# Hybrid mLSTM, sparse attention and retention block: the low part of a weight chunk made by two engines, one k-tile each

## The chip, the cores and the metric

One core of one Trainium2 chip runs the whole program. Time is device time in microseconds (us) of one launch, median of three runs. The engines named here: PE does matmuls, DVE elementwise work, reductions and top-k steps, ACT activations and copies, POOL (GpSimd) elementwise work, and SP issues most DMAs.

## What is computed

Two layers on x of 512 tokens by 1024 features, all in float32. Cut to the sections that matter here:

```
z = rms_norm(x) @ w_in                       # split into q,k,v,i,f,o (mLSTM), latents (attention),
                                             # q,k,v,g (retention), three gates
hm = mlstm(silu(conv(q,k)), v, i, f)         # chunks of 128 tokens, a state carried along
idx = sum_g w_idx[g] * relu(q_idx[g] @ k_idx)    # 8 indexer heads; the top 128 keys of each query
ha = attention over the chosen keys, with a bucketed bias
hr = retention(rotary(q), rotary(k), v)      # chunks of 128, a state carried along
y = sig(g_m)*(hm@p_m) + sig(g_a)*(ha@p_a) + sig(g_r)*(hr@p_r)
x = x + y @ w_out;  x = x + (silu(h@w_gate) * (h@w_up)) @ w_down
```

## The kernel before

Activations stay on the chip; weights are streamed. Every product is made from a high and a low part of both factors, three matmuls for one (`mm3`, L251 to L253: high by high, high by low, low by high). A weight chunk is two k-tiles of 128 rows by up to 512 columns. `chunk` (L221 to L235) loads it from HBM into `raw` (two buffers) by a DMA that SP issues, lets ACT make the high part `whi` by a copy to the reduced float type (L233), and lets DVE subtract it from `raw` for the low part `wlo` (L234); `whi` and `wlo` have three buffers each. A full chunk feeds 24 matmuls of 512 columns.

The layer goes through sections of four chunks each (`feat_section`, `tok_section`): latents and gates first, then qk, mv (the values of the mLSTM), mo (its output gate), rq, rk, rv, rg of the retention, then the gates, output projections and the FFN. Work of other kinds is fed between the matmuls by generators (`during`, `tick`): the indexer runs beside qk and mv, `conv_silu` and `mlstm_gates` beside mv, `mlstm_pre` and `topk` beside mo, `mlstm` and `topk` beside rq to rg, `retention` from the first gate section on. The names for later: `qs` is an indexer query split in its high and low part (ACT L605, DVE L606), `relu` is ACT's evacuation of the indexer's scores (L629), `mask` the sum over heads (DVE L634); `topk` takes 16 rounds of MAX8 and MATCH_REPLACE8 over each of three masks (L649, L650) and ends a mask at L652; `msc` and `mst` (DVE L852, L862) belong to the mLSTM's steps, `rsc` (DVE L911) to the retention's; `sm` and `mm` are PSUM tiles. POOL multiplies gains (L468, L549, L550), and finishes rotary (L524, L525).

What stands in which order on an engine's queue is decided when the program is built: a scheduler walks an estimate of the program and takes the ready instruction of the highest priority. Weight chunks are made under high priority (`tc.high_priority` in `chunk`), the top-k rounds under a low one (`TOP_PRIO`). So a change of an instruction's size or engine also changes the order of others. Once built, each engine runs its queue strictly in order.

Of the kernel before, what the change touches and what calls it, by code (L numbers as in the profile page):

```python
# [11 lines left out]
F32 = mybir.dt.float32  # L12
# [91 lines left out]
class Block:  # L104
    def __init__(self, ctx, tc, a, depth):
        self.tc, self.nc, self.a, self.depth = tc, tc.nc, a, depth
        pool = lambda name, bufs, **k: ctx.enter_context(tc.tile_pool(name=name, bufs=bufs, **k))
        self.const = pool("const", 1)
        self.wp = pool("wp", 3)
        self.big = pool("big", 1)  # L110
        self.wk = pool("wk", 1)
        self.st = pool("st", 4)
        self.ps = pool("ps", 1, space=PSUM)
        self.dram = pool("dram", 1, space=DRAM)
        self.feed = []
        self.ahead = []
        self.late = []

    def tick(self):
        for f in self.feed:  # L120
            f[2] += f[1]
            while f[2] >= 1.0:
                f[2] -= 1.0
                next(f[0], None)
# [98 lines left out]
    def chunk(self, k0, kt, parts, width, offset=None):  # L223
        nc = self.nc
        with self.tc.high_priority(offset=offset):
            raw = self.wp.tile([128, 2, 512], F32, name="raw", tag="raw", bufs=2)
            hi = self.wp.tile([128, 2, 512], F32R, name="whi", tag="whi")
            lo = self.wp.tile([128, 2, 512], F32R, name="wlo", tag="wlo")
            for c0, src in parts:
                n = src.shape[1]  # L230
                nc.sync.dma_start(raw[:, 0:kt, c0:c0 + n], src.rearrange("(k p) c -> p k c", p=128))
            r, h, o = (t[:, 0:kt, 0:width] for t in (raw, hi, lo))
            nc.scalar.activation(h, r, AF.Copy)  # L233
            nc.vector.tensor_sub(o, r, h.bitcast(F32))  # L234
        return hi, lo  # L235

    def chunks(self, w, cols, rows=None):
# [138 lines left out]
    def mixer(self, l, act):  # L376
        nc, a = self.nc, self.a
# [46 lines left out]
        for h in range(4):  # L424
            o = 64 - 64 * (h % 2)
# [9 lines left out]
        def conv_silu():  # L435
            for f, z in enumerate(pre_conv):
# [12 lines left out]
                    nc.vector.tensor_mul(kT[f - 2], y, z)  # L449
                yield  # L450

        masks = {b: self.r(f"mask{b}", [128 * (b + 1)]) for b in range(1, NT)}
        idx = self.indexer(l, anorm, CT, wgt, masks)
        bias = self.bias_table() if l == 0 else iter(())
# [99 lines left out]
        ret = self.retention(rq, rk, rv, rg, hr)  # L554
        self.tok_section(w_in, ((C_RG, C_RG + 512),), act, ev_rg)
        self.drain(top)
        att = self.attention(l, CT, masks, haT)
        self.during((ret, 1.25))
        sg = gate(C_GM, 0)
# [279 lines left out]
    def mlstm(self, qz, kT, v1, og, hmT):  # L839
# [6 lines left out]
        def chunk(c):  # L846
# [39 lines left out]
            self.to_T(hx, hmT, c)  # L886

        yield from wave(chunk(c) for c in range(NT))

    def retention(self, rq, rk, rv, rg, hrT):  # L890
# [5 lines left out]
        def chunk(c):  # L896
# [38 lines left out]
            self.to_T(hx, hrT, c)  # L935

        yield from wave(chunk(c) for c in range(NT))

    def ffn(self, l, X, act):
# [94 lines left out]
```

## Time and profile before

| | us |
|---|---|
| three runs | 1827.42, 1827.93, 1828.56 (median 1827.93) |
| profiled execution | 1827.7 |
| its span | 1825.9 |
| TensorE clock granted | 0.999 of full speed over the span |

The profiled execution's own time is 1.8 us longer than its span. Rows of a timeline are one instruction or several alike in a run (x2), with the start in us from the beginning of the span and the time; a bracket gives the idle time of the engine ahead of it and what ended it. Two-input instructions are TENSOR_TENSOR and SCALAR_TENSOR_TENSOR. The figures of PE's matmuls overlap: a 512-column matmul shows as 0.39, and starts follow each other every 0.227 us.

### The profile page before, as it was taken

How to read it: one execution, taken by the hardware profiler on the slowest of the kernel's cores; microseconds unless marked ns; L12 is line 12 of the kernel's file. 1: busy time of each engine (PE TensorE's matmuls, PEld its weight loads, DVE VectorE, ACT ScalarE, POOL GpSimd, SP SyncE). 2: the span in 40 equal slices, each digit the busy share in tenths (PEclk: the TensorE clock that was granted, in tenths of full speed). 3: DMA queues.
4: the chain of work that ended last, by engine and by line, in shares of the span. 5: the costliest groups of instructions: out<-in, count | busy, mean ns of one | idle time of the engine just before them, and what ended most of it. 6: DMA issues, size and time to landing. Idle time of an engine off the chain costs nothing.

```text
span 1825.9 us, 22880 instructions
## 1 busy us (share of the span) xinstructions
PE 1796.5 (98%) x8720; PEld 1490.9 (82%) x8720; DVE 982.5 (54%) x1798; ACT 741.1 (41%) x1208; POOL 217.5 (12%) x274
## 2 busy tenths in 40 slices
PE   9999999999999999999999999999999999999998
PEld 6878888888888888888887788888888888888886
DVE  5698985455545333322357999744546443333223
ACT  5572235656434323322246523365654333223221
POOL 3112140121000000000020122301210000000000
PEclk9999999999999999999999999999999999999999
DMA  5622423222235333322342233232223253332232
GB/s 187 202 86 77 116 69 100 93 85 87 82 126 161 93 95 102 92 97 100 102 131 70 75 91 95 71 113 74 90 70 138 83 156 97 93 104 92 94 102 81
DMA packets 126845, 185.95 MB, mean 102 GB/s; under 512 B 12256, under 2 KB 71136, under 8 KB 126736
## 3 DMA queue, kind: packets, MB, share of 16 engines
q1 hardware_dynamic: 125408, 178.98, 31.4%
q0 software_dynamic: 1184, 5.26, 0.9%
q8 instruction: 68, 1.11, 0.2%
q14 instruction: 41, 0.34, 0.1%
q10 hardware_dynamic: 144, 0.26, 0.0%
HBM read 177.64 MB, written 6.84 MB: 101 GB/s over the span
## 4 chain that ended last, share of the span: by engine, by line
PE 78%; DVE 14%; ACT 3%; DMA 2%; issue 2%; POOL 1%; SPq 0%; POOLq 0%; ACTq 0%; DVEq 0%
PE mm L251 23%; PE mm L253 23%; PE mm L252 23%; DVE wlo L234 3%; DVE mask L650 3%; DVE top L649 2%; PE sm L731 2%; PE sm L710 1%; ACT whi L233 1%; PE sm L724 1%; DMA raw<-w_up 1%; DVE ru L523 1%; PE sm L369 1%; DVE mhx L362 0%; DMA uk<-a_wuk 0%
## 5 line engine op out<-in xcount | busy, mean ns | idle before, releaser
L234 DVE TENSOR_TENSOR wlo<-raw,whi 128x1024 fp32r<-128x1024 f32 (+2 forms) x302 | 374.2, 1239 | 590.6 <-ACT whi L233 590.3
L233 ACT ACTIVATE whi<-raw 128x1024 fp32r<-128x1024 f32 (+2 forms) x302 | 314.0, 1040 | 716.8 <-PE mm L252 300.8
L251 PE MATMUL mm<-hT,whi 128*128 128x512 f32 (+1 forms) x1216 | 465.9, 383 | 0.4 <-ACT rg L544 0.2
L252 PE MATMUL mm<-hT,whi 128*128 128x512 f32 (+1 forms) x1216 | 460.5, 379 | 1.0 <-DVE hT L304 1.0
L253 PE MATMUL mm<-hT,wlo 128*128 128x512 f32 (+1 forms) x1216 | 460.9, 379 | 0.0
L253 PEld LDWEIGHTS mm<-hT,wlo 128*128 128x128 f32 x1216 | 228.7, 188 | 43.1
L252 PEld LDWEIGHTS mm<-hT,whi 128*128 128x128 f32 x1216 | 229.0, 188 | 41.9 <-DVE hT L304 1.6
L251 PEld LDWEIGHTS mm<-hT,whi 128*128 128x128 f32 x1216 | 228.9, 188 | 41.7 <-ACT rg L544 0.8
L251 PE MATMUL mm<-whi,hT 128*128 128x512 f32 (+1 forms) x448 | 177.2, 396 | 2.0 <-ACT hT L303 1.3
L253 PE MATMUL mm<-whi,hT 128*128 128x512 f32 (+1 forms) x448 | 174.6, 390 | 0.0
L252 PE MATMUL mm<-wlo,hT 128*128 128x512 f32 (+1 forms) x448 | 174.1, 389 | 0.0
L251 PEld LDWEIGHTS mm<-whi,hT 128*128 128x128 f32 x448 | 84.1, 188 | 19.5 <-ACT hT L303 2.0
L253 PEld LDWEIGHTS mm<-whi,hT 128*128 128x128 f32 x448 | 84.1, 188 | 18.1 <-issue 1.2
L252 PEld LDWEIGHTS mm<-wlo,hT 128*128 128x128 f32 x448 | 84.2, 188 | 16.0 <-issue 0.5
L321 POOL TENSOR_SCALAR rs<-ms 128x1 f32<-128x1 f32 x16 | 5.7, 355 | 619.0 <-ACT hn L319 619.0
L251 PE MATMUL mm<-whi,fa 128*128 128x512 f32 x192 | 75.5, 393 | 0.0
L252 PE MATMUL mm<-wlo,fa 128*128 128x512 f32 x192 | 75.5, 393 | 0.0
L253 PE MATMUL mm<-whi,fa 128*128 128x512 f32 x192 | 75.4, 393 | 0.0
L712 POOL TENSOR_TENSOR cmb<-tb,mask 128x256 f32<-128x256 f32 (+2 forms) x48 | 51.4, 1074 | 161.2 <-PE sm L724 55.1
L251 PE MATMUL mm<-whi,fr 128*128 128x512 f32 x160 | 62.4, 390 | 0.0
L253 PE MATMUL mm<-whi,fr 128*128 128x512 f32 x160 | 62.3, 389 | 0.0
L252 PE MATMUL mm<-wlo,fr 128*128 128x512 f32 x160 | 62.3, 389 | 0.0
(286 smaller groups left out, 2654.7 us busy)
## 6 DMA issues: line engine op xcount, KB each, us to landing
raw<-w_in SPq DMA_DIRECT2D x104, 512.0 KB, 3.6
raw<-w_gate SPq DMA_DIRECT2D x96, 256.0 KB, 2.8
raw<-w_up SPq DMA_DIRECT2D x96, 256.0 KB, 3.1
raw<-w_down SPq DMA_DIRECT2D x44, 512.0 KB, 3.6
raw<-w_out SPq DMA_DIRECT2D x16, 512.0 KB, 3.6
x<-x SPq DMA_DIRECT2D x8, 512.0 KB, 6.4
rot<-c_rot SPq DMA_DIRECT2D x16, 256.0 KB, 3.2
tb<-bias_dram SPq DMA_DIRECT2D x16, 256.0 KB, 3.9
```

Of the source, the lines that this page charges most:

```text
L233: nc.scalar.activation(h, r, AF.Copy)
L234: nc.vector.tensor_sub(o, r, h.bitcast(F32))
L251: t.matmul(out, lhsT=A[0], rhs=B[0], start=start, stop=False)
L252: t.matmul(out, lhsT=A[0], rhs=B[1], start=False, stop=False)
L253: t.matmul(out, lhsT=A[1], rhs=B[0], start=False, stop=stop)
L369: self.nc.tensor.transpose(p[:, h, :], x[:, h, :], self.ident)
L523: nc.vector.tensor_mul(u, z, sin)
L649: nc.vector.max(m8, acc)
L650: nc.vector.match_replace(acc, m8, acc, TAKEN)
L710: nc.tensor.matmul(p, lhsT=q[v][:, b * 128:(b + 1) * 128], rhs=kk[v][:, 0:SP], start=v == 0, stop=v == 1)
L712: nc.gpsimd.tensor_add(c, tb[:, T - S:T], masks[b] if b else self.neg)
L731: nc.tensor.matmul(o[:, b, :], lhsT=PT[:, s, :], rhs=V[s][:, h * 64:(h + 1) * 64], start=s == 0, stop=s == b)
```

## The change

A flag `share` is set in each layer from before the qk section until the rg section has been issued. While it holds, a chunk of two k-tiles has its low part made in two instructions: DVE subtracts k-tile 0 (128x512), POOL subtracts k-tile 1 (128x512). That concerns 29 chunks of a layer, the four of each of seven sections and the indexer's own weights, 58 in all; the other chunks stay with one DVE instruction.

```diff
--- before.py
+++ after.py
@@ -115,6 +115,7 @@
         self.feed = []
         self.ahead = []
         self.late = []
+        self.share = False
 
     def tick(self):
         for f in self.feed:
@@ -231,7 +232,10 @@
                 nc.sync.dma_start(raw[:, 0:kt, c0:c0 + n], src.rearrange("(k p) c -> p k c", p=128))
             r, h, o = (t[:, 0:kt, 0:width] for t in (raw, hi, lo))
             nc.scalar.activation(h, r, AF.Copy)
-            nc.vector.tensor_sub(o, r, h.bitcast(F32))
+            n = 1 if self.share and kt == 2 else kt
+            nc.vector.tensor_sub(o[:, 0:n], r[:, 0:n], h[:, 0:n].bitcast(F32))
+            if n < kt:
+                nc.gpsimd.tensor_sub(o[:, n:kt], r[:, n:kt], h[:, n:kt].bitcast(F32))
         return hi, lo
 
     def chunks(self, w, cols, rows=None):
@@ -449,6 +453,7 @@
                     nc.vector.tensor_mul(kT[f - 2], y, z)
                 yield
 
+        self.share = True
         masks = {b: self.r(f"mask{b}", [128 * (b + 1)]) for b in range(1, NT)}
         idx = self.indexer(l, anorm, CT, wgt, masks)
         bias = self.bias_table() if l == 0 else iter(())
@@ -554,6 +559,7 @@
         ret = self.retention(rq, rk, rv, rg, hr)
         self.tok_section(w_in, ((C_RG, C_RG + 512),), act, ev_rg)
         self.drain(top)
+        self.share = False
         att = self.attention(l, CT, masks, haT)
         self.during((ret, 1.25))
         sg = gate(C_GM, 0)
```

Line numbers of the new kernel lie above those of the old: by 1 from L115, by 4 from L235, by 5 from L452, by 6 from L557.

The change also moves instructions. Four places follow, rows of the old kernel first, then of the new one. On DVE in layer 1, beside the mv section, where the last indexer pair is made (`qs`; `cy` and `qz` are the convolution, `g` are gate rows):

```order
L790 TENSOR_SCALAR g_727<-g_727 4x128
L441 SCALAR_TENSOR_TENSOR cy<-cz,conv,cy 128x511
L234 TENSOR_TENSOR wlo<-raw,whi 128x1024
L634 SCALAR_TENSOR_TENSOR mask_434<-relu,wgt,mask_434 128x256
L634 SCALAR_TENSOR_TENSOR mask_435<-relu,wgt,mask_435 128x384
L606 SCALAR_TENSOR_TENSOR qs<-sm,qs 64x384
L234 TENSOR_TENSOR wlo<-raw,whi 128x1024
```

```order
L236 TENSOR_TENSOR wlo<-raw,whi 128x512
L640 SCALAR_TENSOR_TENSOR mask_436<-relu,wgt,mask_436 128x512
L793 SCALAR_TENSOR_TENSOR g_733<-g_733,g_ms 4x128
L451 SCALAR_TENSOR_TENSOR qz<-cy,cz 64x512 x2
L236 TENSOR_TENSOR wlo<-raw,whi 128x512
L794 TENSOR_TENSOR g_ms<-g_732,g_733 4x1
L795 TENSOR_SCALAR g_732<-g_733,g_ms 4x128
L796 TENSOR_SCALAR g_733<-g_733 4x128
L640 SCALAR_TENSOR_TENSOR mask_434<-relu,wgt,mask_434 128x256
L640 SCALAR_TENSOR_TENSOR mask_435<-relu,wgt,mask_435 128x384
L640 SCALAR_TENSOR_TENSOR mask_436<-relu,wgt,mask_436 128x512
L612 SCALAR_TENSOR_TENSOR qs<-sm,qs 64x384
```

The first `qs` of the last pair stood behind one whole low part and the masks of the 256- and 384-wide block; it now stands behind two halves, six masks (the first two stand just above the rows shown), two `qz` and the scan steps. On PE, before the group of matmuls that reads this `qs` (`CT` is the transposed latent, `hT` the activations):

```order
L251 MATMUL mm<-whi,hT_118 128x512
L252 MATMUL mm<-wlo,hT_118 128x512
L253 MATMUL mm<-whi,hT_120 128x512
L626 MATMUL sm<-CT_220,qs 128x256
L627 MATMUL sm<-CT_221,qs 128x256
```

```order
L256 MATMUL mm<-wlo,hT_118 128x512
L257 MATMUL mm<-whi,hT_120 128x512
L255 MATMUL mm<-whi,hT_118 128x512
L256 MATMUL mm<-wlo,hT_118 128x512
L257 MATMUL mm<-whi,hT_120 128x512
L255 MATMUL mm<-whi,hT_117 128x512
L632 MATMUL sm<-CT_220,qs 128x256
L633 MATMUL sm<-CT_221,qs 128x256
```

Counted over the queue, the group has 13 matmuls of 512 columns more ahead of it than before. On DVE in layer 1 at the last chunks of rg and the first four of the gate section, before the first `rsc`:

```order
L649 MAX top<-mask_436 128x8
L650 MATCH_REPLACE mask_436<-top,mask_436 128x512
L649 MAX top<-mask_436 128x8
L650 MATCH_REPLACE mask_436<-top,mask_436 128x512
L234 TENSOR_TENSOR wlo<-raw,whi 128x1024
L652 TENSOR_SCALAR mask_436<-mask_436 128x512
L234 TENSOR_TENSOR wlo<-raw,whi 128x1024 x2
L911 TENSOR_TENSOR rsc<-sm,cm 128x512
```

```order
L236 TENSOR_TENSOR wlo<-raw,whi 128x512
L655 MAX top<-mask_436 128x8
L656 MATCH_REPLACE mask_436<-top,mask_436 128x512
L655 MAX top<-mask_436 128x8
L656 MATCH_REPLACE mask_436<-top,mask_436 128x512
L658 TENSOR_SCALAR mask_436<-mask_436 128x512
L236 TENSOR_TENSOR wlo<-raw,whi 128x512
L236 TENSOR_TENSOR wlo<-raw,whi 128x1024 x4
L917 TENSOR_TENSOR rsc<-sm,cm 128x512
```

Two rounds of top-k and the mask's end stood between low parts of gate chunks; they now stand ahead of them, and `rsc` follows four whole low parts. On PE in layer 2, where the last indexer group stands beside the mv section:

```order
L253 MATMUL mm<-whi,hT_6645 128x512
L251 MATMUL mm<-whi,hT_6643 128x512
L252 MATMUL mm<-wlo,hT_6643 128x512
L626 MATMUL sm<-CT_7402,qs 128x384
L627 MATMUL sm<-CT_7403,qs 128x384
L626 MATMUL sm<-CT_7402,qs 128x512
L627 MATMUL sm<-CT_7403,qs 128x512
```

```order
L256 MATMUL mm<-wlo,hT_6672 128x512
L257 MATMUL mm<-whi,hT_6674 128x512
L255 MATMUL mm<-whi,hT_6672 128x512
L632 MATMUL sm<-CT_7431,qs 128x384
L633 MATMUL sm<-CT_7432,qs 128x384
L632 MATMUL sm<-CT_7431,qs 128x512
L633 MATMUL sm<-CT_7432,qs 128x512
```

Here the last group of indexer matmuls has 13 matmuls fewer ahead of it.

## Rows read from the trace of the kernel before

**Rows 1.** The page's head and its first part: the span, busy time per engine
```profile
span 1825.9 us, 22880 instructions
...
PE 1796.5 (98%) x8720; PEld 1490.9 (82%) x8720; DVE 982.5 (54%) x1798; ACT 741.1 (41%) x1208; POOL 217.5 (12%) x274
```

**Rows 2.** Waits of PE: who is waited for, us in total, times, longest
```profile
PE sm L926 <- DVE rsc L911: 2.6, 2, 1.6
...
PE sm L626 <- DVE qs L606: 2.2, 2, 1.6
PE sm L626 <- ACT relu L629: 2.1, 2, 1.3
...
PE sm L860 <- DVE mst L862: 1.5, 2, 0.9
...
PE sm L873 <- DVE msc L852: 1.1, 2, 0.9
```

**Rows 3.** Windows of layer 1: length, busy PE, PEld, DVE, ACT, POOL (count), clock, DMA
```profile
84.00:150.00 66.00, 61.22 (x310) 49.05 (x309) 61.34 (x149) 40.39 (x68) 8.63 (x9) 1.00 0.27 79
172.00:242.00 70.00, 69.95 (x326) 57.70 (x326) 69.18 (x138) 24.44 (x34) 25.84 (x22) 1.00 0.40 117
```

**Rows 4.** Groups by line and form: count, busy us, mean ns, idle before
```profile
L234 DVE TENSOR_TENSOR wlo<-raw,whi 128x1024 fp32r<-128x1024 f32 x286 | 360.9, 1262 | 564.5 <-ACT whi L233 564.1
...
L712 POOL TENSOR_TENSOR cmb<-tb,mask 128x512 f32<-128x512 f32 x16 | 20.9, 1307 | 48.4 <-PE sm L710 13.6 <-PE sm L731 9.2 <-DVE y L493 8.6
...
L364 DVE TENSOR_TENSOR mhx<-mhx,og 128x512 f32<-128x512 f32 x8 | 5.5, 682 | 0.0
```

**Rows 5.** Timeline, DVE around the last indexer pair: start, us, engine, line, operation
```profile
90.25 0.47 DVE L787 TENSOR_TENSOR_SCAN g<-g,g_ms 4x128 f32<-4x128 f32 x1
...
91.35 0.67 DVE L789 TENSOR_SCALAR g<-g,g_ms 4x128 f32<-4x128 f32 x1
...
93.07 1.20 DVE L234 TENSOR_TENSOR wlo<-raw,whi 128x1024 fp32r<-128x1024 f32 x1
94.20 0.99 DVE L634 SCALAR_TENSOR_TENSOR mask<-relu,wgt,mask 128x256 f32<-128x256 f32 x2
95.23 0.55 DVE L606 SCALAR_TENSOR_TENSOR qs<-sm,qs 64x384 fp32r<-64x384 f32 x1
```

**Rows 6.** Timeline, PE and DVE just behind that
```profile
95.83 0.39 PE L626 MATMUL sm<-CT,qs 128*128 128x256 f32 x1 [0.67 <-DVE qs L606]
...
96.95 0.75 DVE L634 SCALAR_TENSOR_TENSOR mask<-relu,wgt,mask 128x512 f32<-128x512 f32 x1
...
97.61 0.68 DVE L447 SCALAR_TENSOR_TENSOR qz<-cy,cz 64x512 f32<-64x512 f32 x1
```

**Rows 7.** Timeline of layer 2, relu and the PE group that reads it
```profile
1010.57 1.24 ACT L629 ACTIVATE relu<-sm 128x256 f32<-128x256 f32 x3
...
1010.99 0.44 PE L626 MATMUL sm<-CT,qs 128*128 128x384 f32 x1
```

**Rows 8.** Timeline, end of the r_g section and the first gate chunks
```profile
239.20 3.68 POOL L550 TENSOR_TENSOR rg<-rg,rgs 128x512 f32<-128x512 f32 x2
239.44 2.28 DVE L234 TENSOR_TENSOR wlo<-raw,whi 128x1024 fp32r<-128x1024 f32 x1
...
243.00 2.21 DVE L234 TENSOR_TENSOR wlo<-raw,whi 128x1024 fp32r<-128x1024 f32 x1 [1.27 <-ACT whi L233]
...
245.87 0.38 PE L926 MATMUL sm<-rv,rsc 128*128 128x128 f32 x1 [1.01 <-DVE rsc L911]
```

**Rows 9.** Timeline, the first rotation on POOL and DVE beside it
```profile
174.71 2.86 POOL L524 TENSOR_TENSOR rq<-rq,ru 128x256 f32<-128x256 f32 x1 [3.03 <-DVE ru L523]
...
175.15 0.69 DVE L523 TENSOR_TENSOR ru<-rz,rot 128x512 f32<-128x512 f32 x1
```

**Rows 10.** Timeline of layer 2, tightest weights: low part made, then read by PE
```profile
1126.70 1.21 DVE L234 TENSOR_TENSOR wlo<-raw,whi 128x1024 fp32r<-128x1024 f32 x1
...
1128.67 0.39 PE L252 MATMUL mm<-wlo,hT 128*128 128x512 f32 x1
```

## Prediction

> **What bounds the kernel now.** I read the page's head first: PE is busy in 1796.5 of 1825.9 us, DVE in 982.5, POOL in 217.5 [rows 1]. PE sets the end, and a change that takes no matmul away can gain only where PE stands still. So the waits of PE come second: those released by what DVE makes in the changed stretches, and by `relu`, which DVE's masks and queries drive, are 2.6 (`rsc`), 2.2 (`qs`), 2.1 (`relu`), 1.5 (`mst`) and 1.1 (`msc`) [rows 2], together 9.5 us. No wait for `wlo` is among them. Third, the windows: DVE is busy in 61.3 of 66 us from 84 to 150, and in 69.2 of 70 from 172 to 242 [rows 3], where the top-k fills every gap. There DVE is full, but PE works 70 of 70 us: the top-k is wanted only at the end. The tightest chunk I found has its low part ready at 1126.70 + 1.21 = 1127.91 and read at 1128.67 [rows 10], a slack of 0.76 us; no PE wait hangs on the halving itself.
>
> **The change, part by part.** *The halves.* 58 low parts of 128x1024 at 1.262 us on DVE become 58 of 128x512. The nearest two-input row of that size is 0.682 [rows 4], so 0.58 us each leaves DVE, 33.6 in all. On POOL, 58 of 128x512 come in. The trace has no such subtraction there; a multiply of that size takes 1.307 [rows 4], and beside DVE's two-input work 3.68 for two [rows 8], 1.84 each. I take 1.31, the row with most instances: 76 us more on an engine that is busy 217.5 of 1825.9. The low part is then ready when POOL is, 1.31 after `whi` against 1.26: 0.05 later alone, 0.6 later at the upper end, both under the slack of 0.76. Price on PE: 0, with DVE's gain hidden wherever the top-k or PE's own work is the cover. If POOL is not free when its half is due, the cover goes; that is the last rival.
>
> *What the lock costs.* DVE's `wlo` of 239.44 took 2.28 and that of 243.00 2.21, both beside POOL multiplies [rows 8], against 1.20 at 93.07 [rows 5]: two-input work of the two engines does not run at once, and here DVE paid 1.0. But at 174.71 POOL's first rotation took 2.86 while DVE's instruction of 175.15 ran in its usual 0.69 [rows 9]: there POOL paid. So a half on POOL costs DVE between 0 and 1.31. Against the 0.58 it saves, the balance is between +0.58 and -0.73 per chunk. I take a balance near nothing, nearest to the rows of 174.71, since DVE's queue holds ready two-input work at nearly all times in the first stretch. The Trainium skill ("SBUF — State Buffer", section "Who interferes with whom") says the same and speaks against this change: a DVE operation with two SBUF inputs and a GpSimd one share a port pair under an exclusive lock, and whoever holds it blocks the other wholly. By that rule alone the two halves run one after the other, and the sum would be the first rival's; the rows show the exclusion but put the price on either side.
>
> *The moves.* These decide the sum.
> (a) Last indexer pair in layer 1. Today `qs` runs at 95.23 and PE starts its group at 95.83 after a wait of 0.67, so it asked at 95.16 [rows 5, 6]. Now PE has 13 more matmuls at 0.227 ahead, 2.95 us, and asks at 98.1. On DVE, from 93.07 on, the queue holds before that `qs`: two halves 1.36, six masks 2 x 0.99 + 2 x 0.75, two `qz` 1.36, the scan 0.47, `g` steps 0.67 and some 0.4 (the two shortest, estimated from it), together 7.7 [rows 4 to 6]. So `qs` starts at about 100.8 and ends, with 0.55, at 101.4; PE goes on at 101.5. The wait is 3.4 in place of 0.67: **+2.7**.
> (b) The last indexer group of layer 2. PE starts at 1010.99, 0.42 after `relu` began at 1010.57 [rows 7], just in time; now it asks up to 13 x 0.227 = 2.95 sooner. If DVE and ACT, relieved by the halves ahead (0.58 each), deliver sooner by as much, the cost is 0; if not, 2.95. I take **+2.1**, nearer to what (a) shows of the new order.
> (c) `relu` of layer 1: the halves bring it forward a little, **-0.3** of its share of 2.1, an estimate between 0 and -0.8 (what the longest, 1.3, leaves) [rows 2].
> (d) `msc` and `mst`: 1.1 + 1.5 = 2.6 [rows 2]. They come behind (a) and (b) and go by DVE's clock; a PE that is later by 2.7 and 2.1 finds them ready or nearly so. More rounds of top-k now stand before them, so I leave 0.2: **-2.4** (between 0 and -2.6).
> (e) `rsc`: the wait ends at 245.87 [rows 8] and its partner in layer 2 is 1.6 of the 2.6 [rows 2]. Today the last rounds of top-k and the mask's end stand between low parts of gate chunks, and the last of these runs at 243.00 for 2.21, right before `rsc`. It waits 1.27 for its `whi`, whose load waits for the raw buffer that an earlier low part frees. With the top-k rounds no longer among them these low parts run about 2.6 sooner, by my walk of the queue (an estimate: two rounds of two instructions of 512 columns at about 0.68 each, as in [rows 4]): the last would end at 243.00 - 2.6 + 2.21 = 242.6, and PE asks at 245.87 - 1.01 = 244.86. **-2.6**, between 0 and -2.6.
>
> Sum: 2.7 + 2.1 - 0.3 - 2.4 - 2.6 = -0.5. Made against the profiled execution, 1827.7, that is 1827.2; the median of the runs stands 0.2 above it, so the time is **1827.4**. SP's queue keeps its order; a raw buffer is freed when the slower half is read, 0.05 to 0.6 later, while the DMA share in these windows is 0.27 and 0.40 [rows 3], so I give its loads no price.
>
> **The rivals.**
> *Slower, the lock decides.* Each POOL half blocks DVE for 1.31, and 0.73 per chunk is lost. From 95.8 [rows 6] to the last `mst` some 53 us on there are ten chunks (24 x 0.227 = 5.45 us each): 7.3 us, of which DVE's idle 66.0 - 61.3 = 4.7 [rows 3] absorbs a part. 2.6 per layer reach PE at `mst` and its like, 5.2 in all: 1827.4 + 5.2 = 1832.6; if the top-k is then late enough that `rsc` waits as before, 1835.2. I say 1834. It decides from the point where the mean loss of DVE per half is above 0.58 + 4.7/10 = 1.05. For it: 239.44 and 243.00; against it: 174.71, and that one-input top-k work fills most of DVE from 172 on.
> *Faster, the relief reaches PE.* DVE runs ahead by 0.58 per chunk, four chunks before each of these places give 2.3, and (a) and (b) shrink to nothing since masks and `qs` come that much sooner: -0.3 - 2.4 - 2.6 = -5.3, to 1822.6; with the old `qs` and `relu` waits gone too all 9.5 go, 1818.4. For it: DVE is what these five wait for. Against it: the queue puts the relief into top-k rounds first.
> *Slower, POOL is late.* A half that queues behind a rotation on POOL (2.86 at 174.71 [rows 9]) is ready that much later than DVE's, 2.1 past the slack of 0.76. Two such chunks in each layer give 4 x 2.1 = 8.4, 1835.8. For it: the rq and rk sections put two rotations per tile on POOL. Against it: they come with their tile's evacuation, when chunks made ahead stand in three buffers.
> *The change does nothing on the path*: 1827.93, since PE's 70 of 70 us in the second window [rows 3] cover all of it; against it, PE waits in the first. A measurement can't tell this from my forecast, so both share one chance.
>
> **How the numbers follow.** Chances: forecast or nothing on the path 0.52, relief 0.22, lock 0.18, late POOL 0.08. What a measurement can tell from no change is 0.2%, 3.7 us: below 1824.3 is faster, above 1831.6 slower. Faster holds the relief, 0.22; slower lock and POOL, 0.26; the same 0.52. The forecast's own range, from its bounds (a to e at their ends, and not all at one end at once) is 1823.5 to 1831.5. To leave out 2 in 10 I go to 1821.5, which holds the middle relief and leaves out the full 9.5, and to 1834.5, which holds the lock's first price and leaves out most of late POOL.
>
> **What would show it.** In the new profile: DVE about 30 us less busy, POOL 76 to 107 more (58 x 1.31 to 1.84); `wlo` halves on DVE at 0.68 where alone, on POOL 1.3; a wait of PE for `qs` above 3 us in layer 1; `rsc` gone from the waits; `msc` and `mst` below 0.5. Wrong would be: waits of PE for a `wlo` from POOL (late POOL), DVE halves above 1.6 on the mean (lock), no longer `qs` wait (relief).

## The result, and the profile after

The changed kernel takes 1845.24 us (median of 4 runs, 1843.88 to 1846.62) against 1827.95 in runs of the kernel before beside it: 17.3 us more, a ratio of 1.0096 with a 95% interval of 1.0084 to 1.0108. It is slower, and far outside the range that was forecast. The page's head, to be held against [rows 1]:

```profile
span 1842.5 us, 22990 instructions
...
PE 1801.0 (98%) x8720; PEld 1494.6 (81%) x8720; DVE 979.0 (53%) x1798; ACT 743.5 (40%) x1210; POOL 305.1 (17%) x332
```

DVE is only 3.5 us less busy (982.5 to 979.0), although half of 58 low parts left it. POOL has 87.6 us more. PE has 4.5 us more for the same 8720 matmuls; most of it is time at a lower clock, two stretches of which are shown below. The rest of the 16.6 us of span is waiting. PE's waits, to be held against [rows 2] (engine waited for, us in total, times, longest):

```profile
PE sm L632 <- DVE qs L612: 7.0, 6, 3.2
PE sm L632 <- ACT relu L635: 3.8, 3, 2.1
PE mm L256 <- DVE wlo L236: 3.7, 3, 2.2
PE sm L866 <- DVE mst L868: 3.1, 5, 0.8
...
PE mm L255 <- ACT rv L542: 2.4, 1, 2.4
...
PE sm L879 <- DVE msc L858: 1.2, 2, 0.9
...
PE mm L255 <- ACT rg L549: 0.7, 1, 0.7
```

`rsc` is gone from the list, as forecast. In its place `qs` has 7.0 in place of 2.2, `relu` 3.8 in place of 2.1, `mst` 3.1 in place of 1.5, and three waits are new or grown from next to nothing: `wlo` 3.7, `rv` 2.4 and `rg` 0.7. The groups by line and form have the two halves of the low part, POOL's and DVE's (count, busy us, mean ns, idle before):

```profile
L238 POOL TENSOR_TENSOR wlo<-raw,whi 128x512 fp32r<-128x512 f32 x58 | 97.0, 1676 | 163.0 <-ACT whi L234 159.1 <-ACT g_tok L813 3.7
...
L236 DVE TENSOR_TENSOR wlo<-raw,whi 128x512 fp32r<-128x512 f32 x58 | 56.1, 966 | 20.2 <-ACT whi L234 20.1
```

A half costs DVE 0.966 on the mean where 0.682 was reckoned, and POOL 1.676. The 58 halves so save 17.2 us (58 x (1.262 - 0.966)); the busy time fell by 3.5 only, so 13.7 us went back into other instructions of DVE, which got longer. Together 30.1 of 33.6 us of relief are taken back, 0.52 per half.

Two places show what this does to PE. The first is the last indexer pair of layer 1 (timeline: start, us, engine, line, operation, and in brackets the idle time and its end):

```profile
92.43 2.04 DVE L640 SCALAR_TENSOR_TENSOR mask<-relu,wgt,mask 128x256 f32<-128x256 f32 x2
...
94.99 1.78 DVE L640 SCALAR_TENSOR_TENSOR mask<-relu,wgt,mask 128x512 f32<-128x512 f32 x1
...
99.55 1.66 DVE L640 SCALAR_TENSOR_TENSOR mask<-relu,wgt,mask 128x256 f32<-128x256 f32 x3
101.24 0.55 DVE L612 SCALAR_TENSOR_TENSOR qs<-sm,qs 64x384 fp32r<-64x384 f32 x1
```

The same place in PE's timeline:

```profile
101.84 0.39 PE L632 MATMUL sm<-CT,qs 128*128 128x256 f32 x1 [3.22 <-DVE qs L612]
...
104.03 0.63 PE L257 MATMUL mm<-whi,hT 128*128 128x512 f32 x1
```

And the windows over it (length, busy PE, PEld, DVE, ACT and POOL with their counts, granted clock, DMA share, GB/s):

```profile
98.00:102.00 4.00, 0.78 (x4) 0.35 (x3) 3.91 (x10) 0.18 (x1) 0.00 (x0) 1.00 0.42 121
102.00:103.50 1.50, 1.34 (x7) 0.90 (x8) 1.44 (x4) 1.45 (x3) 0.03 (x1) 1.00 0.12 46
103.50:107.00 3.50, 3.50 (x10) 2.75 (x11) 3.50 (x6) 0.51 (x1) 1.68 (x1) 0.53 0.06 7
107.00:112.00 5.00, 5.00 (x25) 3.95 (x24) 4.97 (x13) 4.61 (x9) 0.00 (x0) 0.99 0.33 103
```

Three masks and then `qs` are the last that DVE runs while PE stands for 3.22 us. The two masks of 92.43 took 2.04 where the same two took 0.99 before [rows 5], and the one of 94.99 took 1.78 against 0.75 [rows 6]; each time a half on POOL ran beside them, and 2.1 us are lost ahead of this `qs`. PE restarts at full clock, and 1.9 us later its granted clock is at the lower of its two levels, 1.2 GHz: 0.53 of full speed over 103.5 to 107, where a 512-column matmul starts every 0.43 us and shows as 0.63. That is another 1.7 us, half of 3.4. In the changed sections it happens once more, from 1127.7 on, behind a wait of 2.17. (A third such stretch of 3.4 us begins at 11.55, ahead of the changed sections; the profile before has none there.) Two other waits of nearly the same length, 2.35 before 223.68 and 2.13 before 1020.21, were not followed by it.

In PE's timeline of layer 2 the wait before 1020.21 reads:

```profile
1020.21 0.44 PE L632 MATMUL sm<-CT,qs 128*128 128x384 f32 x1 [2.13 <-ACT relu L635]
```

And the one behind which the clock fell, at the first chunk of layer 2's rg section:

```profile
1127.69 0.79 PE L256 MATMUL mm<-wlo,hT 128*128 128x512 f32 x1 [2.17 <-DVE wlo L236]
```

The second place is in layer 1 where the rv section ends and the rg section begins, here in the timeline of ACT, DVE, POOL, PE and SP's queue:

```profile
208.11 1.06 ACT L234 ACTIVATE whi<-raw 128x1024 fp32r<-128x1024 f32 x1 [5.67 <-DMA raw<-w_in]
...
214.79 0.68 DVE L656 MATCH_REPLACE8 mask<-top,mask 128x512 f32<-128x512 f32 x1
...
215.25 2.98 POOL L238 TENSOR_TENSOR wlo<-raw,whi 128x512 fp32r<-128x512 f32 x2
...
215.38 1.71 DVE L236 TENSOR_TENSOR wlo<-raw,whi 128x512 fp32r<-128x512 f32 x1
...
217.01 0.68 DVE L655 MAX8 top<-mask 128x8 f32<-128x512 f32 x1
...
217.14 0.50 PE L256 MATMUL mm<-wlo,hT 128*128 128x512 f32 x1 [0.93 <-DVE wlo L236]
217.15 6.12 SPq L232 DMA_DIRECT2D raw<-w_in  x2
...
222.09 1.06 ACT L234 ACTIVATE whi<-raw 128x1024 fp32r<-128x1024 f32 x1 [5.55 <-DMA raw<-w_in]
...
223.05 0.58 ACT L542 ACTIVATE rv<-mm 128x512 f32<-128x512 f32 x1
...
223.68 0.50 PE L255 MATMUL mm<-whi,hT 128*128 128x512 f32 x1 [2.35 <-ACT rv L542]
```

The low part that PE wants, of rg's first chunk, belongs to the high part of 208.11, ready at 209.2. On DVE it starts only at 215.38: rounds of top-k stand before it, the last of them at 214.79. It takes 1.71 beside POOL's half, and PE waits 0.93. POOL's half of the same chunk comes as late, at 215.25, but is ready first. DVE's low part also holds its raw buffer, so the next load is issued at 217.15, the next high part waits 5.55 us for it until 222.09, and the last evacuation of `rv`, which stands behind that high part on ACT, frees its PSUM tile 2.35 us after PE wanted it. One late low part costs PE twice.

### The profile page after: what moved, and what is told of

It reads as the page before. It is cut to its first block, busy times and chain, and to the rows that moved or that the text cites. A ratio compares the mean times of both kernels' runs of the same rounds, so it can differ in the third digit from the quotient of the medians.

```text
span 1842.5 us, 22990 instructions
## 1 busy us (share of the span) xinstructions
PE 1801.0 (98%) x8720; PEld 1494.6 (81%) x8720; DVE 979.0 (53%) x1798; ACT 743.5 (40%) x1210; POOL 305.1 (17%) x332
## 4 chain that ended last, share of the span: by engine, by line
PE 80%; DVE 13%; ACT 2%; DMA 2%; issue 2%; POOL 1%; SPq 0%; POOLq 0%; ACTq 0%; DVEq 0%
PE mm L255 24%; PE mm L257 24%; PE mm L256 23%; DVE wlo L236 2%; DVE mask L656 2%; DVE top L655 2%; PE sm L737 2%; PE sm L716 1%; PE sm L730 1%; ACT whi L234 1%; DVE ru L528 1%; DVE mask L640 1%; PE sm L373 1%; PE sm L350 1%; DMA raw<-w_up 1%
## 5 line engine op out<-in xcount | busy, mean ns | idle before, releaser
L236 DVE TENSOR_TENSOR wlo<-raw,whi 128x1024 fp32r<-128x1024 f32 (+3 forms) x302 | 356.9, 1182 | 607.4 <-ACT whi L234 602.5
L238 POOL TENSOR_TENSOR wlo<-raw,whi 128x512 fp32r<-128x512 f32 x58 | 97.0, 1676 | 163.0 <-ACT whi L234 159.1
L257 PEld LDWEIGHTS mm<-whi,hT 128*128 128x128 f32 x448 | 85.1, 190 | 17.2 <-DVE hT L308 0.3
```

Of the source, the lines that this page charges most:

```text
L236: nc.vector.tensor_sub(o[:, 0:n], r[:, 0:n], h[:, 0:n].bitcast(F32))
L238: nc.gpsimd.tensor_sub(o[:, n:kt], r[:, n:kt], h[:, n:kt].bitcast(F32))
L257: t.matmul(out, lhsT=A[1], rhs=B[0], start=False, stop=stop)
```

## The experiments

Each kernel ran beside the kernel before on the same chip; ratios are to it, with their 95% interval. Where an order is "held", every instruction of PE, DVE, ACT and SP gets an ordering edge to the one ahead of it in the wanted queue (POOL's stays free), so that what is computed and what stands where can be changed apart:

```diff
+        follow(nc, tc)     # for a, b in zip(order, order[1:]):
+                           #     tc.add_manual_dep(rows[b], rows[a].name, NoSync)
```

The theory that I set out to test is "order": the queues are written for a DVE that is 33.6 us lighter, and it isn't. The rival is "lock": POOL's halves delay what PE waits for, whatever the order.

**The split in the old order.** The changed kernel with its queues held in the order of the kernel before.

> The split of the changed kernel, with the queues of PE, DVE, ACT and SP held in the order of the kernel before. Theory 'order' (the time is lost because the queues were ordered for a DVE that is 33.6 us lighter, so that top-k rounds and masks stand ahead of low parts and queries that PE then waits for; DVE's busy time fell by only 3.5): 1824 to 1831 us, no PE wait for wlo, the qs wait of layer 1 back under 1 us. Theory 'lock' (POOL's halves hold DVE up and this alone delays what PE waits for, whatever the order): 1840 to 1846 us, PE waits for wlo stay.

Measured: 1827.6 us, ratio 1.0006 (0.9997 to 1.0015). No loss that can be told from none, though POOL makes the same 58 halves and DVE is 977.9 busy, near the changed kernel's 979.0. As "order" expected, no wait for `wlo` is there, but `qs` of layer 1 came down to 1.2 only, over the 1 us expected (waits of PE in this run's profile):

```profile
PE sm L632 <- ACT relu L635: 4.2, 3, 1.7
PE sm L632 <- DVE qs L612: 2.6, 3, 1.2
...
PE sm L866 <- DVE mst L868: 2.1, 3, 1.3
...
PE sm L932 <- DVE rsc L917: 0.6, 1, 0.6
```

**Whole low parts in the new order.** The kernel before, held in the order of the changed one.

> The kernel before (DVE makes whole low parts, nothing added on POOL), with the queues of PE, DVE, ACT and SP held in the order of the changed kernel. Theory 'order': at least as slow as the changed kernel, 1843 to 1856 us, with the qs wait near 3 us and waits for wlo, since DVE has no relief at all here. Theory 'lock': 1826 to 1831 us, since no POOL half is there to hold DVE.

Measured: 1839.5 us, ratio 1.0075 (1.0062 to 1.0087). The order alone, with no half on POOL, costs 13 us of the 17. It is less than "order" expected (1843 or more): without the split DVE has no relief in this order, but no lock either. DVE is busy for 977.1 us here, against 979.0 in the changed kernel: in the new order the split takes nothing off DVE. The waits of PE in its profile, those for `wlo` among them:

```profile
PE sm L626 <- DVE qs L606: 5.2, 5, 2.3
PE sm L860 <- DVE mst L862: 3.4, 3, 1.2
...
PE mm L252 <- DVE wlo L234: 1.5, 3, 0.7
```

**The lock alone.** Whole low parts on DVE, old order, and POOL makes the second half again for nobody:

```diff
-            nc.vector.tensor_sub(o[:, 0:n], r[:, 0:n], h[:, 0:n].bitcast(F32))
+            nc.vector.tensor_sub(o, r, h.bitcast(F32))
             if n < kt:
-                nc.gpsimd.tensor_sub(o[:, n:kt], r[:, n:kt], h[:, n:kt].bitcast(F32))
+                ...                                     # dup: a tile of 128x512 that nobody reads
+                nc.gpsimd.tensor_sub(dup, r[:, n:kt], h[:, n:kt].bitcast(F32))
```

> DVE makes whole low parts in the order of the kernel before, and POOL makes the second k-tile's low part a second time into a tile that nobody reads: the lock without any relief. Theory 'order': DVE busy rises by 25 to 35 us (0.4 to 0.6 per POOL half), spread over 58 places, and the time by 3 to 9 us, 1831 to 1837. Theory 'lock': 1845 us or more, as in the changed kernel or worse, since DVE is given nothing back.

Measured: 1846.9 us, ratio 1.0109 (1.0095 to 1.0122). Its page has, by engine:

```profile
PE 1800.8 (98%) x8720; PEld 1492.1 (81%) x8720; DVE 1007.9 (55%) x1798; ACT 740.2 (40%) x1208; POOL 322.4 (18%) x332
```

DVE has 25.4 us more than before, 0.44 per POOL half, as expected; but the time rose by 20 us, not by 3 to 9, to where "lock" had put it. Here "order" as I had put it fell, and the lock is no minor matter: of 25 us that are taken from a DVE that is full, 20 reach the end.

**The relief alone.** DVE makes the first half; the second is left out and the high part is read in its place (that part of the result isn't computed); nothing on POOL; old order.

```diff
-            if n < kt:
-                nc.gpsimd.tensor_sub(o[:, n:kt], r[:, n:kt], h[:, n:kt].bitcast(F32))
-        return hi, lo
+        return hi, Low(lo, hi) if n < kt else lo      # Low, not shown, reads hi for k-tile 1
```

> DVE makes the first k-tile's low part only; the second k-tile's is left out and its high part read in its place (that part of the result is not computed), nothing on POOL, queues in the order of the kernel before. What the split could give without the lock in the old order. Both theories: DVE busy 33 us less; by 'order' PE's waits for rsc, qs, relu, mst and msc, 9.5 us, shrink by 3 to 8 us: 1820 to 1825. If DVE's relief reaches no wait of PE: 1827 to 1829.

Measured: 1816.7 us, ratio 0.9948 (0.9935 to 0.9960), 9.8 us faster, more than expected. The busy times of its page:

```profile
PE 1793.6 (99%) x8720; PEld 1493.2 (82%) x8720; DVE 951.0 (52%) x1798; ACT 742.2 (41%) x1208; POOL 212.0 (12%) x274
```

DVE is 31.5 us lighter, and of the five waits of [rows 2] only 3.2 us are left. So DVE's load does set PE's time here, and the split would have been worth about 10 us if POOL's half had been free. With the first run this gives the lock its price inside the split: DVE 951.0 to 977.9, 0.46 per half, and the time from 0.9948 to 1.0006, some 11 us.

**The relief alone in the new order.** The same edit, held in the order of the changed kernel.

> As the run with the relief alone (DVE makes the first k-tile's low part, the second's is left out and its high part read in its place, nothing on POOL), but with the queues in the order of the changed kernel. Theory 'order for a lighter DVE' (the new order is as good as the old for a DVE that really is 33 us lighter, and loses only because the lock takes the relief back): 1815 to 1820 us, no waits for wlo, as with the relief in the old order (1816.7). Rival 'order bad in itself' (masks and top-k rounds stand where PE waits for what is behind them, at any speed of DVE): 1824 to 1832 us, with the qs wait of layer 1 above 1.5.

Measured: 1822.9 us, ratio 0.9978 (0.9969 to 0.9987): between the two. `qs` of layer 1 waits 1.8 for the pair that waited 1.6 before [rows 2] and 1.2 for the last pair, on either side of the rival's mark, and no wait for `wlo` is there. So the new order is some 6 us worse than the old even for a DVE that is lighter, and adding the lock to it costs far more, from 0.9978 to 1.0096, some 21 us, twice what it costs in the old order. Neither theory alone holds: the order is worse, and it has less room for the lock. The waits of PE that are left in this run's profile:

```profile
PE sm L638 <- DVE qs L618: 3.4, 4, 1.8
...
PE sm L638 <- ACT relu L641: 2.6, 4, 1.5
...
PE sm L872 <- DVE mst L874: 1.9, 3, 0.8
```

**Top-k as before.** The changed kernel, only top-k rounds and low parts on DVE held in their old sequence to each other.

```diff
+        follow(nc, tc)     # DVE alone, rows of L234, L649, L650 and L652 of the kernel before
```

> The changed kernel, with only the top-k rounds and the low parts on DVE held in the sequence they have to each other in the kernel before; the rest of DVE and the other engines are ordered freely. Theory 'top-k' (in the rk to rg sections low parts come late since eight to nine more rounds of top-k stand ahead of each): the waits for wlo and for the rv and rg evacuations in the new profile, 0.9 + 2.4 + 2.2 + 0.6 + 0.7, and one stretch of half clock, some 1.7, go; rsc's 2.6 may come back: 1835 to 1840 us. Theory 'masks' (the indexer's stretch holds nearly all of the loss): 1842 to 1846.

Measured: 1833.9 us, ratio 1.0040 (1.0027 to 1.0052): of 17 us, 10 are back, somewhat more than expected. No wait for `wlo` is left, and `rsc` came back with 0.4 only (waits of PE):

```profile
PE sm L632 <- DVE qs L612: 5.6, 6, 1.8
...
PE mm L255 <- ACT rv L542: 0.9, 1, 0.9
...
PE sm L932 <- DVE rsc L917: 0.4, 1, 0.4
```

What remains is mostly the indexer's stretch, where `qs` (5.6) and `relu` (4.6) together wait nearly as long as in the changed kernel (10.2 against 10.8); `mst` also stays at 3.1. So the place of low parts among top-k rounds is the larger part of the loss, masks ahead of `qs` the smaller.

**The split in half of the sections.** With `share` set from qk to mo only, and from rq to rg only:

```diff
         self.drain(pre)
+        self.share = False          # qk to mo only; for rq to rg: share = True here, not before qk
```

> The split in the indexer's weights and the qk, mv and mo sections only, ordered freely. From the waits of the two profiles (84 to 160 and its twin in layer 2: 15.2 us after, 7.2 before) and one stretch of half clock of some 1.7: +9 to +10, 1835 to 1839 us, if the two stretches are independent ('additive'). Rival: the second stretch inherits DVE's lateness from the first, and this alone already gives 1842 or more.

> The split in the rq, rk, rv and rg sections only, ordered freely. 'Additive': the waits of the new profile there (wlo, rv, rg: 7 us) and a stretch of half clock of some 1.7, less rsc's 2.6: +4 to +6, 1831 to 1834 us. Rival 'inherits': the rounds of top-k are ahead only because the first stretch was split too, so this gives 1826 to 1829.

Measured: qk to mo 1834.0 us, ratio 1.0040 (1.0026 to 1.0054); rq to rg 1836.4, ratio 1.0050 (1.0038 to 1.0063). The sum, 0.0090, agrees with the whole change's 0.0096 within the intervals: the two stretches add up, and "inherits" falls. But the shares were off, and both times lie outside what was expected: the first cost 7 us where 9 to 10 were expected, the second 9.4 where 4 to 6 were. In the second, PE also waits 3.6 us for `mst`, in place of 1.5, and a wait for the half on POOL, 0.2 us, is seen for once (waits of PE, rq to rg only):

```profile
PE sm L866 <- DVE mst L868: 3.6, 5, 1.1
...
PE mm L256 <- POOL wlo L238: 0.2, 1, 0.2
```

**POOL writes only.** As the lock alone, but POOL fills the unread tile three times with zeros behind each high part.

```diff
...                                                     # DVE makes whole low parts, as in the lock alone
+                for _ in range(3):
+                    m = nc.gpsimd.memset(dup, 0.0)      # each after the high part, by an edge not shown
-                nc.gpsimd.tensor_sub(dup, r[:, n:kt], h[:, n:kt].bitcast(F32))
```

> As the run with the lock alone (DVE makes whole low parts, order of the kernel before), but in place of the duplicate subtraction POOL fills the unread tile three times with zeros, each time after the same high part is done: POOL about as long busy (3 x 0.53), but it reads nothing from SBUF. If it is POOL's reading that holds up DVE's two-input instructions: DVE busy within 3 us of 982.5 and the time within 0.2% of before, 1825 to 1830 us. If POOL's being busy or its writing is enough: DVE busy up by 15 to 30 us and 1835 to 1847 us.

Measured: 1827.2 us, ratio 1.0005 (0.9996 to 1.0014). By engine its page reads:

```profile
PE 1796.0 (98%) x8720; PEld 1491.7 (82%) x8720; DVE 982.0 (54%) x1798; ACT 741.1 (41%) x1208; POOL 304.9 (17%) x448
```

POOL is as busy as in the changed kernel (304.9), DVE is at 982.0, and nothing is lost. So neither POOL's being busy nor its writing holds DVE up; what the subtraction does besides is to read SBUF.

**Moving nine instructions instead.** The kernel before, without a split, with `rsc` of both layers, two `qs`, `msc` and two `mst` on DVE and two `relu` on ACT a few places ahead in held queues. The first of the nine, on DVE in layer 1 and 2:

```diff
-wlo, wlo, rsc
+wlo, rsc, wlo
...
-wlo, wlo, rsc
+rsc, wlo, wlo
```

> The kernel before, no split, with nine instructions moved ahead in its queues: on DVE rsc of both layers ahead of one or two low parts, two qs, msc and two mst ahead of masks, top-k or statistics, on ACT two relu ahead of a high part or a gate activation. Theory 'order' (PE's waits in these stretches are set by queue positions, not by DVE's load): of the 9.5 us of waits 5 to 8 go, 1819 to 1823 us, without any relief of DVE. If DVE's load sets them, the waits reappear behind the moved instructions: 1825 to 1829.

Measured: 1824.1 us, ratio 0.9985 (0.9976 to 0.9994), between what the two theories expected. It beats both kernels, the one before by 0.15%. The waits for `rsc` are gone (2.6 us), those for `mst` and `msc` went from 2.6 to 1.7; others came back one step further on, so the gain is short of the 5 to 8 expected (waits of PE in its profile):

```profile
PE sm L626 <- DVE qs L606: 1.7, 2, 1.6
...
PE sm L626 <- ACT relu L629: 1.2, 2, 0.7
PE sm L251 <- ACT relu L629: 1.1, 1, 1.1
```

**The split with the same moves.** The changed kernel, held in the reordered queues.

> The split, with the queues in the order of the kernel before and the same nine instructions moved ahead as in the reordered kernel before (1824.1). If the split is worth nothing in any order that PE does not wait on: 1823 to 1827 us. If DVE's small net relief (4.6 us in the run with the split in the old order) helps once the waits are moved: 1819 to 1822. If the lock falls on the moved instructions: 1827 or more.

Measured: 1827.4 us, ratio 1.0002 (0.9993 to 1.0011). With the moves too the split gains nothing; it lies where the expectation had put a lock that falls on the moved instructions, if barely, and PE waits 1.7 us there for the `qs` of layer 1 that had been moved ahead, against 0.2 without the split. That is one profile's wait; whether the lock caused it was not tested.

## Why the prediction was wrong

Step by step, as the prediction put it:

- **The halves, "price on PE: 0".** This is the step that failed. I reckoned when a low part is ready after it has begun (0.05 to 0.6 us later, slack 0.76 [rows 10]) and never where DVE's half now stands in its queue. In the rk to rg sections low parts began some 5 to 6 us after their high part already, and were ready 0.8 to 3.6 us ahead of PE. Seven to nine more rounds of top-k for most of them, counted along the queue, were put ahead; now they begin up to 8.3 us after, and the margin of the chunks that aren't late is down to 0.2 to 3: the half of 215.38 has a high part that was ready at 209.2. `wlo` 3.7, `rv` 2.4 and `rg` 0.7 us come from there, together 6.8 where 0.5 stood before and 0 was priced, and one of the stretches at the lower clock. Holding only the top-k in its old place gave 10 of the 17 us back, so this is the larger part of what the sum missed.
- **What the lock costs, "a balance near nothing".** Right in size: 0.52 per half against 0.58 saved, where the range was 0 to 1.31; in the old order relief and lock cancel to 1.0006, and in the new one DVE is as busy with the split (979.0) as with whole low parts (977.1). But I let this zero stand as a cost of nothing in an order that was written for a relief of 0.58. The new profile was to show DVE 30 us less busy; that contradicted the balance, and I did not see it. POOL's half is 1.676, nearer to the upper end (1.84) than the 1.31 that I took.
- **(a) the last indexer pair of layer 1**: the number is right, in part by luck. `qs` was to start at 100.8 and PE to go on at 101.5 after 3.4; it started at 101.24, and PE went on at 101.84 after 3.22. But the working had it from the order alone, with DVE's instructions at their usual length, and 2.1 us of it were lost by the masks beside POOL's halves. In the same order without a half on POOL the wait here is 0.80 (whole low parts) and 1.16 (relief alone), first and second row:

```profile
101.18 0.39 PE L626 MATMUL sm<-CT,qs 128*128 128x256 f32 x1 [0.80 <-DVE qs L606]
...
99.60 0.39 PE L638 MATMUL sm<-CT,qs 128*128 128x256 f32 x1 [1.16 <-DVE qs L618]
```

- **(b) the last indexer group of layer 2**: right, 2.13 for +2.1. With the relief alone in the new order it is 0.44, near the 0 that was named for a DVE that really is relieved. Not priced were three `qs` waits in this stretch of layer 2, 1.1, 0.2 and 0.5 us.
- **(c) `relu` of layer 1, "-0.3"**: right in sign; its wait of 0.8 is gone, though one of 0.2 is new at an earlier pair. The sum rose to 3.8 by (b) and because the wait in layer 2's qk section grew from 1.25 to 1.48.
- **(d) `msc` and `mst`, "-2.4"**: wrong, 2.6 to 4.3. A late PE does not find them ready, since DVE is later still. With the top-k in its old place they are 3.3, in the new order with the relief alone 2.1: the lock and the top-k rounds both have a part in it.
- **(e) `rsc`, "-2.6"**: right, the waits are gone, and in the way forecast: the low parts ahead of `rsc` in layer 1 begin 0.03 us after their high parts.
- **The clock** was in no term: two stretches of 3.4 us at the lower level in the changed sections, 1.7 us each.

Summed from the waits: `qs` +4.8, `relu` +1.7, `msc` and `mst` +1.7, `wlo` +3.7, `rv` and `rg` +2.6 (both stood at 0.5 in sum before), `rsc` -2.6, together 11.9; with 4.5 of PE's own, of which the clock's two stretches are 3.4, that is 16.4, and other waits of PE add 0.4 in sum, against 16.6 us of span: the account closes within 0.2 us. Of the rivals, "the lock decides" was the nearest, but not by its mechanism: it asked for a loss above 1.05 per half and got 0.52. "POOL is late" was wrong in its price: POOL's halves did come late (that of 215.25 starts 6 us after its high part), but where PE waited DVE's half was ready later still; where the profile names a wait for POOL's it is 0.2 us, in one experiment. None of the three signs of being wrong that the prediction named showed up; what told was that DVE was 3.5 us less busy, not 30, and that `msc` and `mst` stood at 4.3, not below 0.5.

The Trainium skill ("SBUF — State Buffer", section "Who interferes with whom") has it that a DVE instruction with at most one SBUF input does not contend with GpSimd, unless it runs in a mode that uses both of DVE's ports, and that one with two inputs contends with a GpSimd instruction that reads SBUF but not with one that only writes. The runs agree: the one-input top-k step of 217.01 takes its 0.68 beside POOL's halves of 215.25, DVE's two-input half of 215.38 takes 1.71 beside them, and with POOL writing only DVE stays at 982.0. Yet not all one-input work went free. The TENSOR_SCALAR that ends a mask reads one tile; beside POOL's halves of 1124.46 it took 1.29, against 0.35 on the mean in the kernel before (last row). Whether it ran in such a mode no run shows.

```profile
1124.46 2.63 POOL L238 TENSOR_TENSOR wlo<-raw,whi 128x512 fp32r<-128x512 f32 x2
...
1124.68 1.29 DVE L658 TENSOR_SCALAR mask<-mask 128x384 f32<-128x384 f32 x1
...
L652 DVE TENSOR_SCALAR mask<-mask 128x384 f32<-128x384 f32 x2 | 0.7, 346 | 0.0
```

Not settled: what share of the 21 us between the new order with relief alone and the whole change falls on low parts and what on queries and masks under the lock; the experiments part these by sections and by top-k, not by the lock in each. Nor is it settled how much of the 20 us of the lock alone comes through DVE: POOL's subtraction also keeps the raw buffer until it has read it, which the zeros don't, and ACT waited 63.8 us for loads into `raw` from `w_in` there, against 38.1 before and 49.0 with the zeros.

## What to carry to other kernels

Before work is shared between two engines, ask what both read: here POOL's reading of SBUF held up DVE's two-input work and some of its one-input work, and 30 of 33.6 us of relief were taken back. Where a scheduler orders the queues by its own estimate, a change of work is also a change of order, and the two can be measured apart by holding the order; in this case the split in the old order was worth nothing, and with the new order it cost 16 us more. When checking whether data come in time, count from where the producer now stands in its queue, not from when it used to begin.

## What the runs showed of the hardware that was not expected

- The price of the lock is not one or the other side's alone: a POOL half of 128x512 took 1.68 on the mean, where 30 of the 58 took 1.25 to 1.31, and cost DVE 0.44 (lock alone), 0.46 (split in the old order) or 0.56 us (new order, 979.0 less 946.8 over 58).
- What a held-up instruction of DVE lost did not go by its own size: beside a POOL half a scan of 4x128 took 1.51 at 1008.38 in place of 0.47 [rows 5], and a mask of 128x512 took 1.78 at 94.99 in place of 0.75 [rows 6], about 1 us each.
- A wait of 3.22 and one of 2.17 us were followed by 3.4 us at the lower clock, the first only after 1.9 us of work at full clock; waits of 2.35 and 2.13 were not. With the top-k as before such a stretch followed a wait of 1.79 for the first `qs` of layer 1, and in the changed kernel none followed a wait of 1.79 at the same place. A wait of PE can so cost 1.7 us more than its length; its length alone did not tell which one would.
- POOL writing zeros for 92 us more beside the same work cost DVE and PE nothing that could be measured.
